# One column block of the mix projection moved ahead of the query, key and value weights in the first half of a prompt: a decoder step on one Trainium2 core

## The chip, the cores and the metric

The program runs on one core of a Trainium2 chip. A core has a TensorE (PE in the profile), a VectorE (DVE), a ScalarE (ACT), a GpSimd (POOL) and a SyncE (SP, which here only issues transfers), each with an instruction stream of its own that it works through in order. The metric is the device time of one execution in microseconds (us); lower is better.

## What is computed

One layer of a hybrid decoder, for a prompt of 1024 tokens and for 8 sequences of 8 new tokens whose attention reads a paged cache of 8192 tokens each. Cut to the parts that matter here:

```
n = rmsnorm(h, g_mix);  u = n @ w_in                       # 1024 -> 1968 columns
gq, gk, gv, gg, ga, mq, mkv, mkr = split(u, [256, 256, 512, 512, 16, 256, 128, 32])
o_gla = gated linear attention of gq, gk, gv, gates from ga; times silu(gg)
qf  = rmsnorm(mq)  @ mla_w_qup     # 256 -> 8 heads x 96, then norms and rope
k,v = rmsnorm(mkv) @ mla_w_kvup    # 128 -> 8 heads x 128
o_mla = attention of the prompt (causal), or of the new tokens over their cached pages
h = h + concat(o_gla, o_mla) @ w_o
h = h + convolutional gated MLP(rmsnorm(h))
h = h + (p @ ple_w_proj) * sigmoid(rmsnorm(h, g_ple) @ ple_w_gate)
```

All of it is float32; matrix products are made of three products of high and low parts (`mm3`, L161), so each weight is cast to a high part (on ACT, L138) and has that subtracted for a low part (L139, on DVE or POOL).

## The kernel before

The program interleaves two streams of work. `cache_stream` (L705) goes over 64 blocks of cached pages. `dense` (L1379) does the prompt: two calls of `prompt_half` (512 tokens each), then the gated linear attention, then the prompt's own attention. The loop at L1636 takes a step from one or from the other: each step of `dense` yields an estimate of its length, and a step of the cache stream is taken whenever its own running sum (4.4 times a factor of `PACE`) is behind. After that a scheduler of the language places the instructions of each engine, so that the two streams are woven together instruction by instruction; a change in the order of the steps therefore moves rows far beyond its own place.

Inside `prompt_half(hf)`, the opening transposes the normed prompt rows into `xTh`, `xTl`, computes the latent columns (`proj_lat`, rows `ps_lt`, kept in `lat`), and, in the first half alone, also the samples' queries: `sample_q` and `q_finish` (L333) turn the product `ps_qs` into normed, rotated queries `qt`; `sample_absorb` transposes those (`pt_q`, L439), multiplies by `WkT` (`ps_qp`, L443) and transposes the rotary part (`pt_qr`, L449). The cache stream can only start when `qp` and `qr` are there.

Then come the parts that the change touches, at L965 to L976:

- `mix(chunks)` (L883): for each column block of 128 columns, `load_mix` reads it in two transfers of 256 KB (`stage<-w_in`), ACT casts both, POOL subtracts both (`lo_eng=pool`). `proj` makes 24 matmuls of 128x512 (`ps_pj`, 8 each of L162, L163 and L164) and ACT copies the sum out (L753). `post` sends it to memory (L850) and, in the first half, makes the samples' columns: 8 matmuls `ps_sm` (L309), an ACT copy (L312), two DVE additions (L313, L315), a transpose (`pt_gvs`, L854) and its copy (L855).
- `rank` transposes the 16 gate columns (`pt_ga`, L869); `norm_latents` norms the latents (L323 on ACT, L131 and L134 on POOL, L326 to L329 and L198 to L201 on DVE).
- `load_q` reads the query weights in four transfers of 192 KB (`stage<-mla_w_qup`), `load_kv` the key and value weights in two of 256 KB (`stage<-mla_w_kvup`); ACT casts them and DVE, not POOL, subtracts (L139, 128x384 and 128x512).
- For each of the four row tiles: `latents_T` (`pt_cq`, L925), then the next column block of `PLAN`, then `heads` (products `ps_q` and `ps_kv`, the norms, and the stores `dq`, `dk`, `dv`).

All weights go through a ring of three buffers named `stage`: a transfer waits until the ACT cast and the subtraction that read the buffer three loads earlier are done. The split weights stand in three buffers `w`; the query weights hold two of them (`wpair`) until the last `heads` of a half.

Of the kernel before, what the change touches and what calls it, by code (L numbers as in the profile page):

```python
# [26 lines left out]
DFF = 2816  # L27
PACE = [1.41, 1.088, 1.601, 1.168, 1.142, 0.708, 1.035, 1.027]
SP = 50
PLAN = ([0], [], [1, 2, 3])  # L30
EARLY = tuple((u // 2, u % 2) for u in range(9))
PASSAGE = (
# [35 lines left out]
def step_kernel(ctx: ExitStack, tc: tile.TileContext, A):  # L68
# [199 lines left out]
    def load_q():  # L268
        return [wload(wp, A["mla_w_qup"][0][:, f * 384:(f + 1) * 384], 2, 384, "w", sbufs=3, out=wpair(2, 384))
                for f in range(2)]  # L270
# [5 lines left out]
    def load_mix(c0, lo_eng=pool):  # L276

        w = wtile().rearrange("p (k s c) -> p k s c", k=8, s=2)
        hl = wload(wp, w_in[:, c0:c0 + P], 8, P, "w", sbufs=3, lo_eng=lo_eng, out=(w[:, :, 0], w[:, :, 1]))
        return hl + (w,)  # L280
# [460 lines left out]
    def prompt_half(hf):  # L741
# [5 lines left out]
        def proj(w, n, st=None):  # L747
            ps = pd([P, 512], "ps_pj")
            for k in range(8):
                mm3(ps[:n], w[0][:, k, :], w[1][:, k, :], xTh[:, k, :], xTl[:, k, :], k == 0, k == 7)  # L750
            if st is None:
                st = wk.tile([P, 512], F32, tag="st", name="st", bufs=3)
            act.copy(st[:n], ps[:n])  # L753
            return st
# [79 lines left out]
        def gates(G, G0):  # L834

            with tc.high_priority():
                for x in [G, ggs] + G0:
                    tc.keep_in_program_order(act.activation(x, x, AF.Silu))
                tc.keep_in_program_order(act.preload_act_table_set("natural_log_exp_and_others"))
            put_gates(G, hs)  # L840
            for x, t in zip(G0, (0, 256)):
                put_gates(x, slice(t, t + 256))
# [4 lines left out]
        def post(c, st, w, G=None):  # L847
            c0 = c * P
            if c < 4:
                sp.dma_start(dgqk[c0:c0 + P, hs], st)  # L850
            if hf == 0:
                t = proj_sample(w, pd)
                pt = pd([P, 512], "pt_gvs")
                pe.transpose(pt[:, :R], t, ident[:R, :R])  # L854
                act.copy(gqT[:, c, :] if c < 4 else ggs[:, c - 8, :], pt[:, :R])  # L855
                if c == 11:
                    put_gates(G, hs)
            elif c == 8:
                for t in (0, 256):
                    x = wk.tile([P, 4, 256], F32, tag="xin", name="G0")  # L860
                    sp.dma_start(x, dgg[:, t:t + 256].rearrange("(c p) t -> p c t", p=P))
                    G0.append(x)
# [3 lines left out]
        def rank():  # L866
            pt = pd([P, 4, P], "pt_ga")
            for i in range(4):
                pe.transpose(pt[:16, i], lat[:, i, 0:16], ident)  # L869
            ga = wk.tile([P, 512], F32, tag="st", name="ga", bufs=3)  # L870
            act.copy(ga[:16], pt[:16].rearrange("p i c -> p (i c)"))
            sp.dma_start(dga[1:17, hs], ga[:16])
            sp.dma_start(dga[0, hs].rearrange("(a b) -> a b", a=4), ones64[0:4])

        def norm_latents(i):
            t = 4 * hf + i
            tt = slice(t * P, (t + 1) * P)
            l = lat[:, i, 16:NL]
            latents(l, P, ropep[:, t, :], l[:, 0:256], l[:, 256:384], l[:, 384:416])
            sp.dma_start(A["ckv_p"][tt, :], l[:, 256:384])  # L880
            sp.dma_start(A["krope_p"][tt, :], l[:, 384:416])

        def mix(chunks, G=None):  # L883
            prev = None
            for c in chunks + [None] * bool(chunks):
                if c is not None:
                    w = load_mix(c * P)
                    st = proj(w, P, G[:, c - 8] if c >= 8 else None)
                    if c == 11 and hf > 0:
                        gates(G, G0)  # L890
                if prev is not None:
                    post(*prev, G)
                prev = (c, st, w)
                yield (5.3 if hf else 7.2) if c is not None else 0.3
# [27 lines left out]
        def latents_T(i):  # L922
            pt = pd([P, 4, P], "pt_cq")
            for c in range(3):
                pe.transpose(pt[:, c, :], lat[:, i, 16 + c * P:16 + (c + 1) * P], ident)  # L925
            cTh = wk.tile([P, 3, P], F32R, tag="u", name="lTh")
            cTl = wk.tile([P, 3, P], F32R, tag="lTl", name="lTl", bufs=1)
            split(cTh, cTl, pt[:, 0:3])
            return cTh, cTl
# [32 lines left out]
            sp.dma_start(dv[tt, :], vt.rearrange("p h c -> p (h c)"))  # L962
            yield 1.3

        yield from mix(PLAN[0])  # L965
        rank()
        for i in range(4):
            norm_latents(i)
        yield from mix(PLAN[1])
        wq = load_q()  # L970
        wkh, wkl = load_kv()
        for i in range(4):
            cT = latents_T(i)
            yield from mix(PLAN[2][i:i + 1])
            yield from heads(i, *cT)
        z["part"] = 2 * hf + 1  # L976
        values(0)
# [401 lines left out]
    def dense():  # L1379
        for hf in range(2):  # L1380
            z["part"] = 2 * hf
            if hf:
                z["gla"] = gla_weights()
            yield from prompt_half(hf)
        den.close()
        wa2 = const.tile([17, 256], F32, tag="gtile", name="wa2")
        sp.dma_start(wa2[0:1], A["gla_b_a"])
        sp.dma_start(wa2[1:17], A["gla_w_a2"][0])
        with ExitStack() as s2:
            g, g2 = (s2.enter_context(tc.tile_pool(name=nm, bufs=2, reuse_waits="tile")) for nm in ("g", "g2"))  # L1390
            z["part"] = 4
            sample = gla_sample(g, wa2, *z["gla"])
            for n, w in enumerate(gla_prompt(g2, wa2, *z["gla"])):
                yield w
                if n > GS0:
                    z["part"] = 5
                    w2 = next(sample, None)
                    if w2 is not None:
                        yield w2
            for w in sample:  # L1400
                yield w
        with ExitStack() as s2:
            ap = s2.enter_context(tc.tile_pool(name="ap", bufs=2, reuse_waits="tile"))
            z["part"] = 6
            yield from prompt_attention(ap)
        z["part"] = 7
        wo_room()
# [1438 lines left out]
```

## Time and profile before

| | us |
|---|---|
| median of 3 runs | 2199.56 (2196.43 to 2205.49) |
| profiled execution, device time | 2198.96 |
| its span in the trace | 2197.3 |
| DVE busy | 1704.0 (78%) |
| ACT busy | 1384.2 (63%) |
| POOL busy | 1229.4 (56%) |

A row of the timeline reads: start, time taken, engine, line, operation, output and input tile with shapes, count; in square brackets the idle time of the engine before it and who ended that. A row of the windows reads: the stretch, its length, busy time of each engine with the number of instructions, then the TensorE clock granted (1.00 is full), the share of the transfer engines and their rate. Transfers in the first 110 us, among them the weights in question, are issued by SP in the order of the program; that order, and the other engines', can be listed from the built program without times.

### The profile page before, as it was taken

The numbers are of one execution on the slowest core, as the hardware profiler recorded it, in microseconds if no ns is written. First come the engines' busy times: TensorE is split into PE (matmuls) and PEld (weight loads), VectorE is DVE, ScalarE is ACT, GpSimd is POOL, SyncE is SP. The second block draws the span as 40 slices with busy tenths as digits, with TensorE's granted clock in tenths as the row PEclk, the third lists the DMA queues.
The fourth block names the chain that finished last, engine by engine and source line by source line (L and its number), as shares of the span: only waits on it lengthen the run. The fifth ranks groups of instructions, "written<-read, shape, count | busy, mean of one in ns | idle before, by whom it ended". The sixth has DMA issues, their size and how long they took to land. (4 is left out here: it accounts for less than half of the span.)

```text
span 2197.3 us, 37407 instructions
## 1 busy us (share of the span) xinstructions
PE 2121.5 (97%) x12928; PEld 1901.9 (87%) x12928; DVE 1704.0 (78%) x2611; ACT 1384.2 (63%) x3735; POOL 1229.4 (56%) x1348
## 2 busy tenths in 40 slices
PE   7999999999999999999999999999999999999998
PEld 6888978878888888887898978999999999888787
DVE  4775667377778888887788888788888886887795
ACT  5676766777778888887777776443333334434761
POOL 6675668576677777767454656556566562011211
PEclk9999999999999999999999999999999999999999
DMA  5343245422342222221431223232322325778642
GB/s 184 109 142 111 72 124 159 131 70 61 104 125 65 61 68 66 62 62 42 164 91 61 68 74 118 90 110 82 98 91 93 100 92 193 221 219 245 195 145 84
DMA packets 203576, 244.55 MB, mean 111 GB/s; under 512 B 42940, under 2 KB 137260, under 8 KB 203388
## 3 DMA queue, kind: packets, MB, share of 16 engines
q1 hardware_dynamic: 184428, 181.39, 26.3%
q0 software_dynamic: 17728, 56.31, 8.7%
q10 hardware_dynamic: 1232, 4.46, 0.6%
q8 instruction: 104, 1.70, 0.3%
q14 instruction: 84, 0.69, 0.1%
HBM read 196.39 MB, written 45.67 MB: 110 GB/s over the span
## 5 line engine op out<-in xcount | busy, mean ns | idle before, releaser
L583 ACT ACTIVATE csq<-ks 128x256 f32<-128x256 f32 x1040 | 392.8, 401 | 93.7 <-PE ks L164 82.0
L588 DVE TENSOR_REDUCE css<-csq 128x16 f32<-128x1024 f32 (+1 forms) x264 | 315.7, 1196 | 60.4 <-ACT csq L583 59.2
L138 ACT CAST wh<-st 128x512 fp32r<-128x512 f32 x164 | 100.9, 619 | 169.9 <-PE ps_gu L163 157.6
L162 PE MATMUL ks<-mv0h,cTh 128*128 128x320 f32 (+1 forms) x520 | 171.5, 332 | 7.4 <-ACT sn L585 3.7
L162 PE MATMUL ks<-mv1h,cTh 128*128 128x320 f32 (+1 forms) x520 | 170.1, 329 | 7.6 <-ACT sn L585 3.6
L628 POOL TENSOR_TENSOR chl<-craw,chl 128x1024 fp32r<-128x1024 f32 x64 | 141.5, 2211 | 55.4 <-ACT chl L626 54.8
L163 PE MATMUL ks<-mv1l,cTh 128*128 128x320 f32 (+1 forms) x520 | 153.8, 298 | 0.0
L163 PE MATMUL ks<-mv0l,cTh 128*128 128x320 f32 (+1 forms) x520 | 152.7, 295 | 0.0
L164 PE MATMUL ks<-mv0h,cTl 128*128 128x320 f32 (+1 forms) x520 | 148.2, 298 | 0.9 <-DVE cTl L139 0.8
L164 PE MATMUL ks<-mv1h,cTl 128*128 128x320 f32 (+1 forms) x520 | 148.4, 299 | 0.1
L656 POOL TENSOR_TENSOR phl<-sn,phl 128x512 fp32r<-128x512 f32 (+1 forms) x63 | 84.0, 1334 | 83.1 <-ACT phl L653 82.6
L139 DVE TENSOR_TENSOR wl<-st,wh 128x512 fp32r<-128x512 f32 x124 | 108.6, 879 | 25.8 <-ACT wh L138 25.7
L139 POOL TENSOR_TENSOR wl<-st,wh 128x512 fp32r<-128x512 f32 x40 | 62.0, 1550 | 104.9 <-ACT wh L138 100.1
L163 PE MATMUL ps_dn<-o 128*128 128x512 f32 x308 | 120.2, 390 | 0.1
L164 PE MATMUL ps_dn<-o 128*128 128x512 f32 x308 | 120.2, 390 | 0.0
L139 DVE TENSOR_TENSOR cTl<-ctp,cTh 128x512 fp32r<-128x512 f32 (+1 forms) x136 | 90.0, 662 | 37.5 <-ACT cTh L138 36.5
L162 PEld LDWEIGHTS ks<-mv0h,cTh 128*128 128x128 f32 x520 | 98.6, 190 | 21.4 <-ACT sn L585 8.1
L585 ACT COPY sn<-ks 128x64 f32<-128x64 f32 x520 | 116.8, 225 | 0.0
L162 PEld LDWEIGHTS ks<-mv1h,cTh 128*128 128x128 f32 x520 | 99.3, 191 | 19.8 <-ACT sn L585 7.4
L1333 POOL TENSOR_TENSOR pl<-p,ph 128x512 fp32r<-128x512 f32 (+1 forms) x96 | 97.5, 1020 | 32.7 <-DVE ph L1332 22.7
L162 PE MATMUL ps_dn<-o 128*128 128x512 f32 x308 | 115.8, 391 | 0.0
L164 PE MATMUL ps_gu<-xrh,wl 128*128 128x320 f32 x352 | 108.8, 309 | 0.0
(744 smaller groups left out, 7760.9 us busy)
## 6 DMA issues: line engine op xcount, KB each, us to landing
raw<-ds SPq DMA_DIRECT2D x77, 256.0 KB
raw<-ffn_w_down SPq DMA_DIRECT2D x66, 256.0 KB
stage<-w_in SPq DMA_DIRECT2D x48, 256.0 KB
wr<-ffn_w_down SPq DMA_DIRECT2D x44, 256.0 KB
st<-ffn_w_gate SPq DMA_DIRECT2D x42, 256.0 KB
st<-ffn_w_up SPq DMA_DIRECT2D x42, 256.0 KB
ds<-cv SPq DMA_DIRECT2D x19, 512.0 KB
oraw<-doT SPq DMA_DIRECT2D x16, 256.0 KB
```

The source lines that it names most:

```text
L138: cast = act.copy(hi, src)
L139: res = (lo_eng or dve).tensor_tensor(lo, src, hi.bitcast(F32), ALU.subtract)
L162: pe.matmul(ps, ah, bh, start=first, stop=False)
L163: pe.matmul(ps, ah, bl, start=False, stop=False)
L164: return pe.matmul(ps, al, bh, start=False, stop=last)
L583: act.activation(sq[:, f * 256:f * 256 + 256], ks[:, 0:256], AF.Square)
L585: act.copy(o.sn[:, g0 + i, :], ks[:, 256:320])
L588: dve.tensor_reduce(o.ss[:, g0 + i + 1 - n:g0 + i + 1, :].rearrange("p i h -> p (i h)"), sq2[:, :n].rearrange("p i (h n) -> p (i h) n", n= ...
L628: pool.tensor_tensor(ch[:, c0:c1, 128:256], src, ch[:, c0:c1, 0:128].bitcast(F32), ALU.subtract)
L656: (dve if drain == 2 else pool).tensor_tensor(phl[:, :nt, 64:128], sb, phl[:, :nt, 0:64].bitcast(F32), ALU.subtract)
L1333: pool.tensor_tensor(pl[:, c0:], p[:, c0:], ph[:, c0:].bitcast(F32), ALU.subtract)
```

## The change

`PLAN` says which column blocks of the mix projection stand at three places of `prompt_half`: ahead of `rank`, between the norms of the latents and `load_q`, and one ahead of each `heads`. It was one table for both halves and is now one for each half. The second half keeps its table. In the first, block 1 moves from the first `heads` to the place ahead of `load_q`, and blocks 2 and 3 move up by one tile.

```
-PLAN = ([0], [], [1, 2, 3])
+PLAN = (([0], [1], [2, 3]), ([0], [], [1, 2, 3]))
...
-        yield from mix(PLAN[0])
+        yield from mix(PLAN[hf][0])
         rank()
         for i in range(4):
             norm_latents(i)
-        yield from mix(PLAN[1])
+        yield from mix(PLAN[hf][1])
         wq = load_q()
         wkh, wkl = load_kv()
         for i in range(4):
             cT = latents_T(i)
-            yield from mix(PLAN[2][i:i + 1])
+            yield from mix(PLAN[hf][2][i:i + 1])
             yield from heads(i, *cT)
```

Every engine has the same instructions before and after; only their order differs. Of the 12,692 matmuls and transposes in PE's order, the 219th is the first that differs and the 6,339th, in the prompt's attention, the last, but for some 20 neighbours that change places much later.

On PE, in the opening, right behind the first column block. The names are: `ps_sm` the samples' columns of block 0, `pt_q` the transposed sample queries, `pt_gvs` the transposed samples' columns, `pt_ga` the gate columns, `ps_pj` a column block's product. Before:

```order
L309 MATMUL ps_sm<-w,xTs 128x256 x4
L439 MATMUL pt_q<-ident,qt 64x64 x8
L854 MATMUL pt_gvs<-ident,gsf 128x64
L869 MATMUL pt_ga<-ident,lat 16x128 x4
L925 MATMUL pt_cq<-ident,lat 128x128 x3
L443 MATMUL ps_qp<-qT_s,WkT 128x64 x8
L162 MATMUL ps_pj<-xTh,w 128x512
L163 MATMUL ps_pj<-xTl,w 128x512
```

and after:

```order
L309 MATMUL ps_sm<-w,xTs 128x256 x4
L439 MATMUL pt_q<-ident,qt 64x64 x8
L854 MATMUL pt_gvs<-ident,gsf 128x64
L869 MATMUL pt_ga<-ident,lat 16x128 x4
L162 MATMUL ps_pj<-xTh,w 128x512
L163 MATMUL ps_pj<-xTl,w 128x512
L164 MATMUL ps_pj<-xTh,w 128x512
L162 MATMUL ps_pj<-xTh,w 128x512
```

Block 1 now begins ahead of `pt_cq` and `ps_qp`: 20 rows of `ps_pj` stand ahead of `ps_qp` where none stood. `pt_q`, `pt_gvs` and `pt_ga` keep their places ahead of block 1.

On DVE, at the same place, the difference in the chain that makes the sample queries `qt` (L123 to L351), with the subtractions of the query weights (`w<-stage`, 128x384) and the samples' columns (`gsf`):

```order
-L139 TENSOR_TENSOR w<-stage,w 128x384 x2
+L139 TENSOR_TENSOR w<-stage,w 128x384
 L123 TENSOR_TENSOR nwt<-qrs 64x16
 L124 SCALAR_TENSOR_TENSOR nwt<-nwt,qss 64x16
 L125 SCALAR_TENSOR_TENSOR qrs<-nwt,qrs 64x16
-L139 TENSOR_TENSOR w<-stage,w 128x384
 L350 TENSOR_TENSOR qt<-qt,qrs 64x8x64
 L353 TENSOR_TENSOR qt<-qt,qrs 64x8x32
+L313 TENSOR_TENSOR gsf<-ps_sm,gsf 64x128
 L351 TENSOR_TENSOR qt<-qt,gqk 64x8x64
```

Of four query-weight subtractions ahead of L351 one is left (the first of the four stood a few rows higher up); one addition of the samples' columns is new there.

On POOL, at the same place, with the cast and subtracted low parts of the column blocks (`w<-stage`), copies for the cache stream (`mv1h`, `mv1l`), and the first cache block's low part (`chl`):

```order
 L496 DMA craw<-cache_ckv,idx 128x1024 x2
+L139 TENSOR_TENSOR w<-stage,w 128x4x128
 L454 CAST mv1h<-mv0h 128x256 x2
-L454 CAST mv1l<-mv0l 128x256 x2
+L454 CAST mv1l<-mv0l 128x256
+L139 TENSOR_TENSOR w<-stage,w 128x4x128
+L454 CAST mv1l<-mv0l 128x256
 L131 TENSOR_SCALAR rs_v<-ss_809 128x3
 L628 TENSOR_TENSOR chl<-craw,chl 128x8x128
```

Both low parts of block 1 now stand ahead of `chl`; before, they stood behind it.

More of the change, by code (lines that the diff above doesn't have):

```diff
@@ L29 @@
 SP = 50
-PLAN = ([0], [], [1, 2, 3])
+PLAN = (([0], [1], [2, 3]), ([0], [], [1, 2, 3]))
 EARLY = tuple((u // 2, u % 2) for u in range(9))
@@ L963, in heads @@
             yield 1.3
-        yield from mix(PLAN[0])
+        yield from mix(PLAN[hf][0])
         rank()
@@ L968, in prompt_half @@
             norm_latents(i)
-        yield from mix(PLAN[1])
+        yield from mix(PLAN[hf][1])
         wq = load_q()
@@ L973, in prompt_half @@
             cT = latents_T(i)
-            yield from mix(PLAN[2][i:i + 1])
+            yield from mix(PLAN[hf][2][i:i + 1])
             yield from heads(i, *cT)
```

## The prediction

> **What bounds the kernel now.** I read the page first, for the engine that sets the pace.
>
> ```profile
> span 2197.3 us, 37407 instructions
> PE 2121.5 (97%) x12928; PEld 1901.9 (87%) x12928; DVE 1704.0 (78%) x2611; ACT 1384.2 (63%) x3735; POOL 1229.4 (56%) x1348
> ```
>
> TensorE is busy for 97% of the span. An edit that removes no TensorE work can gain only from the other 75.8 us (2197.3 − 2121.5) and from time in which the clock is throttled. So the second view is PE's idle time: its waits, longest first (what waited, for whom, total, times, longest).
>
> ```profile
> PE pt L155 <- DVE xin_s L148: 8.6, 1, 8.6
> ...
> PE mt L649 <- DVE mt L646: 5.1, 4, 2.6
> ...
> PE pt_q L439 <- DVE qt L351: 3.6, 1, 3.6
> ...
> PE ps_qp L443 <- ACT qT_s L440: 0.9, 1, 0.9
> ```
>
> The first is the wait for the first input, which nothing here moves. The longest single one after it, `pt_q`, stands exactly where the change cuts in. Third, the windows: one for each 3.4 us around that wait, and four that cut the span at its end, at the end of the slow clock, and where, counted in matmuls, PE's order is about the same again.
>
> ```profile
> 53.93:57.33 3.40, 0.00 (x1) 0.00 (x0) 3.33 (x8) 2.52 (x10) 3.24 (x4) 1.00 0.54 185
> 57.33:60.73 3.40, 2.74 (x16) 1.78 (x16) 3.40 (x12) 1.68 (x8) 1.20 (x2) 0.55 0.51 161
> 60.73:64.13 3.40, 2.91 (x14) 2.92 (x14) 3.31 (x12) 2.42 (x6) 3.06 (x5) 0.50 0.20 42
> 64.13:67.53 3.40, 3.40 (x10) 2.71 (x10) 3.12 (x14) 1.11 (x2) 1.68 (x3) 0.50 0.47 121
> 67.53:70.93 3.40, 3.40 (x22) 2.62 (x21) 1.87 (x6) 0.71 (x2) 2.50 (x11) 0.95 0.32 82
> ...
> 57.55:67.54 9.99, 9.06 (x38) 7.38 (x39) 9.63 (x34) 5.21 (x15) 5.76 (x7) 0.51 0.39 108
> 67.54:1010.00 942.46, 911.83 (x6202) 804.96 (x6201) 699.83 (x1182) 729.40 (x2241) 662.82 (x760) 0.99 0.31 92
> 1010.00:2197.30 1187.30, 1158.40 (x6487) 1052.21 (x6485) 965.60 (x1341) 616.18 (x1394) 525.36 (x524) 0.99 0.39 123
> ```
>
> Two things to see. After the empty stretch the granted clock is 0.51 for 9.99 us, so about 2 × 0.49 × 9.99 = 9.8 us at half speed, worth 4.9 us of work. And two of those three windows are not even full (2.74 and 2.91 of 3.40): what PE runs there is sparse. The place thus costs 3.62 us of waiting, 0.93 at `ps_qp`, and 4.9 of clock: 9.4 us, 0.43% of the span. That is nearly all the change can win where it is made.
>
> **The change, part by part.** It adds and removes nothing: 24 matmuls `ps_pj`, 8 `ps_sm` and their casts only move, so the sum starts at 0 and all terms are waits, clock and order.
>
> *The wait at `pt_q`.* By the order lists `pt_q` stays ahead of block 1 on PE, so the new matmuls can't fill this wait; only the DVE chain behind it can shorten it. That chain before:
>
> ```profile
> 52.36 0.56 DVE L139 TENSOR_TENSOR w<-stage,w 128x384 fp32r<-128x384 f32 x1 [2.55 <-ACT w L138]
> 52.83 2.16 DVE L123 TENSOR_TENSOR nwt<-qrs 64x16 f32<-64x16 f32 x1
> 55.03 0.17 DVE L124 SCALAR_TENSOR_TENSOR nwt<-nwt,qss 64x16 f32<-64x16 f32 x1
> ...
> 55.32 0.55 DVE L139 TENSOR_TENSOR w<-stage,w 128x384 fp32r<-128x384 f32 x1
> 55.79 0.68 DVE L350 TENSOR_TENSOR qt<-qt,qrs 64x512 f32<-64x512 f32 x1
> ...
> 56.73 0.68 DVE L351 TENSOR_TENSOR qt<-qt,gqk 64x512 f32<-64x512 f32 x1
> ```
>
> L123 takes 2.16 us where the like-sized L124 takes 0.17. POOL says why:
>
> ```profile
> 45.97 1.31 POOL L139 TENSOR_TENSOR w<-stage,w 128x512 fp32r<-128x512 f32 x1
> ...
> 48.84 1.79 POOL L496 DMA_INDIRECT craw<-cache_ckv,idx  x1 [0.30 <-issue]
> ...
> 52.48 2.49 POOL L628 TENSOR_TENSOR chl<-craw,chl 128x1024 fp32r<-128x1024 f32 x1
> ```
>
> `chl` runs from 52.48 to 54.97 and L123 ends with it, at 54.99. The two hold each other up. In the new order two subtractions of block 1 (1.31 us each by the row at 45.97) stand ahead of `chl` on POOL, which pushes it to about 52.5 + 2.6 = 55.1, and the subtraction at 55.32 leaves the chain; but L313 enters it, and needs ACT's copy of `ps_sm`. ACT:
>
> ```profile
> 52.23 0.21 ACT L122 ACTIVATE qrs<-qrs 64x16 f32<-64x16 f32 x1
> ...
> 53.79 0.51 ACT L138 CAST w<-stage 128x384 fp32r<-128x384 f32 x1 [0.87 <-DMA stage<-mla_w_qup]
> ...
> 54.68 0.58 ACT L753 COPY st<-ps_pj 128x512 f32<-128x512 f32 x1
> ```
>
> Best case: L122 ends at 52.4 as before; the chain runs free and L313 waits for PE's last `ps_sm` (53.9) and a copy of 0.3, so L351 starts near 54.6 and ends at 55.3, against 57.4 (56.73 + 0.68): 2.1 us won. Worst case: the query weight that ACT still casts ahead of L122 lands later, since block 1's two transfers go ahead of it through the three `stage` buffers (it then comes about as late as the cast at 53.79, 1.4 us behind), and `chl` falls into the chain as it does now: L351 near 58.7, 1.3 us lost. What is late next is `pt_gvs`, right behind `pt_q`: it needs DVE's L315, which now has one more query-weight subtraction (0.55) ahead of it, of a load whose `stage` buffer POOL's first subtraction of block 1 must free; so part of the best case would be waited for there again. I take **0.5 won**, the middle, because both ends rest on which of two engines is a few tenths earlier.
>
> [...]
>
> *The wait at `ps_qp`.* It waits 0.93 us for ACT's copy of `pt_q`. Now 20 matmuls of `ps_pj` stand between.
>
> ```profile
> 61.22 3.67 PE L443 MATMUL ps_qp<-qT_s,WkT 64*128 64x64 f32 x16 [0.93 <-ACT qT_s L440]
> ...
> 65.41 0.63 PE L163 MATMUL ps_pj<-xTl,w 128*128 128x512 f32 x1
> 65.83 0.63 PE L164 MATMUL ps_pj<-xTh,w 128*128 128x512 f32 x1
> ...
> 71.07 0.40 PE L162 MATMUL ps_pj<-xTh,w 128*128 128x512 f32 x1
> 71.31 0.40 PE L163 MATMUL ps_pj<-xTl,w 128*128 128x512 f32 x1
> ```
>
> Start to start they take 0.42 us in the slow clock and 0.24 in the full one, so 20 cover 5 to 8 us. ACT's copy now stands behind two casts of query weights, which come two loads later than before; even 4 us more fit under the cover. **0.9 won**; if the cover is gone, 0.
>
> *The clock.* Dense 512-wide matmuls now follow where sparse small ones stood. Other stalls show what a stall costs when dense work follows:
>
> ```profile
> 351.66 0.69 PE L649 MATMUL mt<-ident,bm 64*128 64x64 f32 x2 [2.64 <-DVE mt L646]
> 437.30 0.66 PE L1022 MATMUL ps_z<-wa,gaT 17*128 17x256 f32 x2 [2.42 <-DMA Ss<-state_gla]
> 654.50 0.42 PE L162 MATMUL ks<-mv1h,cTh 128*128 128x320 f32 x1 [1.26 <-ACT cTh L138]
> 350.00:359.00 9.00, 7.34 (x33) 6.93 (x34) 5.64 (x15) 4.61 (x13) 5.53 (x8) 0.62 0.98 286
> 436.00:444.00 8.00, 6.70 (x44) 5.67 (x44) 4.85 (x7) 5.95 (x20) 5.09 (x6) 1.00 0.86 239
> 654.00:660.00 6.00, 5.50 (x30) 4.99 (x31) 4.01 (x8) 3.19 (x11) 5.68 (x7) 0.72 0.76 232
> ```
>
> After the stall at 351.66 the mean of 0.62 over 9 us is 2 × 0.38 × 9 = 6.8 us at half speed. The one of 1.26 us at 654.50 also led to a slow stretch (0.72 in the row from 654 on), while the one of 2.42 at 437.30 did not (1.00). So a stall of about 2.6 us may or may not throttle. I take 6.8 us in place of 9.8, **1.5 won** (half of the 3.0), with 0 and 4.9 as the ends.
>
> *The other queues.* On SP block 1's two transfers pass four of query weights and two of key and value weights, 1.25 MB; those come later by two loads. The last of them and their first use were
>
> ```profile
> 62.02 1.13 ACT L138 CAST wkv<-stage 128x512 fp32r<-128x512 f32 x2
> 76.99 0.45 PE L162 MATMUL ps_q<-w,lTh 128*128 128x384 f32 x1
> ```
>
> so some 14 us lie between, and the first `heads` now stands behind block 2 and more cache work, which covers the two loads; without that cover two late loads would cost PE about 2 us, at the 0.87 that one load costs ACT in the row at 53.79. The rest of ACT's and DVE's opening (L198 to L446, `pt_qr`) is due at block 1's end, 5 to 8 us on.
>
> *The reshuffle.* The order differs on every engine up to about 1010 us. Between 67.54 and there PE idles 942.46 − 911.83 = 30.6 us and loses about 9 to the clock (0.99, rounded): some 40 us in about 20 stalls of 0.5 to 2.6 us, drawn anew. I cost it at **0**, since neither sign follows from any row, and by the spread of 20 such stalls give it 8 us either way.
>
> **Sum.** 0.5 + 0.9 + 1.5 = 2.9 won (ends: 7.9 won, 1.3 lost). The profiled execution took 2199.0 (span 2197.3 and 1.7 around it), 0.6 below the median of 2199.56. 2199.0 − 2.9 = 2196.1; I predict **2196**.
>
> **Rivals.**
> - *The clock stays up.* The stall falls to 1.5 us and PE isn't throttled: all 7.9 won, **2191**. For it: the 2.42 us stall without a slow stretch. Against: the 1.26 us one with it. [...] Chance 0.2.
> - *Nothing won here.* `chl` blocks the chain again, the same wait, the same clock: **2199 to 2200**. For it: the wait stands ahead of the moved block. Chance 0.25.
> - *The reshuffle takes stalls away.* Two of the kind at 351.66 (2.64 plus 3.4 of clock, 6.0) vanish besides the 2.9: **2184**. Chance 0.12.
> - *Slower: the cache stream's maximum comes late.* `mt` (L649) must wait for DVE's L646 in each block. If DVE's woven order puts dense work ahead of L646 in some blocks, each costs those 6.0 us; only 4 waits of this kind exist now. Three more give 2199 − 2.9 + 18 = **2214**; with two it is 2208, still within; the third decides. For it: DVE is 78% busy and its order is drawn anew. Against: there are 4 such waits now, 5.1 us in all. Chance 0.08.
> - The forecast keeps 0.35.
>
> **How the numbers follow.** The local ends (2191 and 2200) with half of the reshuffle's 8 us added give 2187 to 2204; to take in half of what lies between there and the two outer rivals I widen it to **2185 to 2206**. Faster by over 0.5% (about what a measurement of this kernel can tell from no change) means below 2188.6: the reshuffle rival, and a quarter of the first, **0.17**. Slower means above 2210.6: **0.08**. Within: **0.75**.
>
> **What would show it.** In the new profile: the wait `pt_q` between 1.5 and 3.6 us, with L123 short and `chl` behind L351; no wait at `ps_qp`; one slow stretch of about 7 us, with `ps_pj` in it; the stretch from there to about 1010 with idle time of 31 ± 8 us. I am wrong if `pt_q` waits longer than 4 us, if PE waits for `w<-stage` of query weights, or if the gain or loss beyond 8 us lies in the woven part.

## The result, and the profile after

The changed kernel takes 2214.11 us (median of 7 runs, 2210.62 to 2222.16); the one before, run beside it, 2196.97 (7 runs, 2195.19 to 2205.49; the three of the table above are among them). The ratio is 1.0072, 95% interval 1.0051 to 1.0092: slower by some 16 us, where 2196 was forecast and 2206 was the upper end. The profiled execution took 2210.98 us, 12.0 more than that of before. Its page:

```profile
span 2209.0 us, 37427 instructions
PE 2123.2 (96%) x12928; PEld 1902.4 (86%) x12928; DVE 1705.6 (77%) x2611; ACT 1381.1 (63%) x3735; POOL 1228.8 (56%) x1348
```

TensorE is busy for 1.7 us more, and idle for 85.8 us (2209.0 − 2123.2) where it was 75.8. Over the whole span nearly all of the difference is waiting. PE's waits by line, longest first:

```profile
PE ks L162 <- ACT sn L585: 8.7, 14, 1.9
PE pt L155 <- DVE xin_s L148: 8.1, 1, 8.1
PE pt_q L439 <- DVE qt L351: 5.0, 1, 5.0
PE ps_z L1022 <- DMA gaT<-dga: 4.3, 1, 4.3
...
PE mt L649 <- DVE mt L646: 3.9, 3, 2.2
PE o L1341 <- POOL pl L1333: 3.6, 3, 1.6
PE pt_cq L925 <- ACT qt L343: 3.2, 1, 3.2
```

`pt_q` has grown from 3.6 to 5.0, and `ps_qp` is gone from the list. `mt`, the slower rival of the forecast, waits less than before (3.9 against 5.1). `ps_z` waits 4.3 us, for the load of `gaT`, where it waited 2.42 for another load. `o` and `pt_cq` are new in the list. All three stand far behind the place of the change: `pt_cq` at 348 us, `ps_z` at 447, the two longest waits of `o` at 754 and 895.

The opening, on PE, DVE and POOL:

```profile
58.63 1.03 PE L439 MATMUL pt_q<-ident,qt 64*64 64x64 f32 x8 [4.96 <-DVE qt L351]
...
66.35 2.00 PE L443 MATMUL ps_qp<-qT_s,WkT 64*128 64x64 f32 x16
```

```profile
52.49 1.48 DVE L139 TENSOR_TENSOR w<-stage,w 128x384 fp32r<-128x384 f32 x1 [3.29 <-ACT w L138]
53.89 0.36 DVE L123 TENSOR_TENSOR nwt<-qrs 64x16 f32<-64x16 f32 x1
...
54.69 2.67 DVE L350 TENSOR_TENSOR qt<-qt,qrs 64x512 f32<-64x512 f32 x1
...
57.82 0.67 DVE L351 TENSOR_TENSOR qt<-qt,gqk 64x512 f32<-64x512 f32 x1
```

```profile
52.26 1.29 POOL L139 TENSOR_TENSOR w<-stage,w 128x512 fp32r<-128x512 f32 x1
...
54.65 2.17 POOL L628 TENSOR_TENSOR chl<-craw,chl 128x1024 fp32r<-128x1024 f32 x1
```

`chl` did move back on POOL by 2.2 us, as the forecast said, but DVE's chain did not get past ahead of it: DVE's L139, with a subtraction of block 1 beside it on POOL from 52.26 to 53.55, took 1.48 us where the same row took 0.56, and `chl` then falls on L350 (2.67 in place of 0.68), not on L123. The query weight was not late: ACT's L122, behind its cast, stands at 52.37 where it stood at 52.23. The clock, in windows:

```profile
57.07:60.47 3.40, 1.83 (x13) 1.38 (x14) 3.40 (x11) 1.58 (x8) 3.18 (x4) 0.50 0.26 70
60.47:63.87 3.40, 3.40 (x12) 2.77 (x11) 3.34 (x12) 2.41 (x11) 1.10 (x2) 0.67 0.61 169
63.87:67.27 3.40, 3.40 (x19) 2.62 (x19) 2.91 (x18) 0.54 (x1) 1.38 (x2) 1.00 0.45 125
...
58.63:67.00 8.37, 8.37 (x39) 6.47 (x39) 7.85 (x31) 3.72 (x12) 4.18 (x6) 0.76 0.48 128
```

The slow stretch, at the 0.50 that the first of these windows shows, is 2 × 0.24 × 8.37 = 4.0 us, where it was 9.8. At the place of the change itself the sum is thus: `pt_q` 1.3 lost (4.96 − 3.62), `ps_qp` 0.9 won, clock (9.8 − 4.0) / 2 = 2.9 won, together 2.5 won. So the 12 us come from elsewhere. One more landmark: the first `ks` that waits for ACT's `csq` in the prompt's attention, in before and after:

```profile
1061.98 0.41 PE L162 MATMUL ks<-mv0h,cTh 128*128 128x320 f32 x1 [1.37 <-ACT csq L583]
```

```profile
1075.36 0.41 PE L162 MATMUL ks<-mv0h,cTh 128*128 128x320 f32 x1 [1.36 <-ACT csq L583]
```

There the new kernel is 13.4 us late, more than the whole difference of the spans (11.7; the stretch behind this row took 1131 to 1136 us in 19 of the 20 traces, so a difference of 2 us there says nothing). All of the loss is made ahead of about 1060 us, which is the stretch whose order the scheduler has drawn anew; behind it the orders are all but the same. The windows from the end of the slow clock to this row, in before and after:

```profile
67.54:1061.98 994.44, 957.98 (x6478) 843.55 (x6476) 735.03 (x1235) 766.15 (x2340) 699.23 (x803) 0.99 0.30 90
```

```profile
67.00:1075.36 1008.36, 964.31 (x6479) 848.94 (x6477) 736.60 (x1241) 764.60 (x2342) 698.70 (x802) 0.98 0.30 88
```

For the same number of matmuls this stretch takes 13.9 us longer: PE is idle for 7.6 us more (44.1 against 36.5) and busy for 6.3 us more, at a granted clock of 0.98 in place of 0.99, both rounded. So here the loss is waiting in about half, and the rest is the same work taking longer.

### The profile page after: what moved, and what is told of

Same layout as the page of the kernel before. It is cut to its first block, busy times and chain, and to the rows that moved or that the text cites. A ratio compares the mean times of both kernels' runs of the same rounds, so it can differ in the third digit from the quotient of the medians.

```text
span 2209.0 us, 37427 instructions
## 1 busy us (share of the span) xinstructions
PE 2123.2 (96%) x12928; PEld 1902.4 (86%) x12928; DVE 1705.6 (77%) x2611; ACT 1381.1 (63%) x3735; POOL 1228.8 (56%) x1348
## 5 line engine op out<-in xcount | busy, mean ns | idle before, releaser
L628 POOL TENSOR_TENSOR chl<-craw,chl 128x1024 fp32r<-128x1024 f32 x64 | 140.7, 2198 | 50.8 <-ACT chl L626 50.2
L139 DVE TENSOR_TENSOR wl<-st,wh 128x512 fp32r<-128x512 f32 x124 | 108.7, 879 | 26.3 <-ACT wh L138 26.1
L139 POOL TENSOR_TENSOR wl<-st,wh 128x512 fp32r<-128x512 f32 x40 | 62.6, 1564 | 103.0 <-ACT wh L138 103.0
L139 DVE TENSOR_TENSOR cTl<-ctp,cTh 128x512 fp32r<-128x512 f32 (+1 forms) x136 | 90.0, 662 | 31.8 <-ACT cTh L138 31.4
L615 POOL TENSOR_TENSOR sn<-sn,cy 128x512 f32<-128x512 f32 (+1 forms) x64 | 71.2, 1112 | 70.6 <-DVE cy L613 58.9
```

The costliest lines, as they stand in the source:

```text
L139: res = (lo_eng or dve).tensor_tensor(lo, src, hi.bitcast(F32), ALU.subtract)
L615: pool.tensor_tensor(snv, snv, y[:, :nt].rearrange("p i h -> p (i h)").unsqueeze(2).broadcast_to([P, nt * 8, 8]), ALU.mult)
L628: pool.tensor_tensor(ch[:, c0:c1, 128:256], src, ch[:, c0:c1, 0:128].bitcast(F32), ALU.subtract)
```

## The experiments

Two theories stood at the start. W: the later weave, drawn anew, makes the loss. O: the opening makes it. To part them the order of issue was pinned: a kernel is built twice, once with each `PLAN`, the scheduled order of each is read, and a third build, a graft, gets the first CUT instructions in one order and the rest in the other, by a dependency that orders each instruction behind the one before it on its engine and waits for no data. 1000 instructions reach to about 110 us, 4500 to about 446, 6500 to about 583. The edit, on top of the changed kernel, for the first graft (the functions `traced` and `ordered`, which pin and read an order, are left out here):

```
+def build(arrays):
+    head, tail = ordered(arrays, HEAD), ordered(arrays, TAIL)
+    first = set(head[:CUT])
+    return traced(arrays, TRACED, head[:CUT] + [k for k in tail if k not in first])[0]
+TRACED, HEAD, TAIL, CUT = AFTER, AFTER, BEFORE, 1000
```

All times are medians. Each ratio is to the kernel before, run beside it (medians of 2196 to 2200 us), with its 95% interval; it is not the quotient of the two medians, and can differ from that by 0.1%. Pinning by itself costs nothing that these runs can tell: c_chl_last, below, is pinned all through in the order of before, but for one POOL instruction, and takes 0.9996 of its time.

**g_open_after**: the changed opening, before's order behind it.

> A graft. Every engine runs the first 1000 scheduled instructions (about 110 us) in the order of the changed kernel, with block 1 ahead of the loads and blocks 2 and 3 one tile earlier, and all others in the order that they have in the kernel before. Theory W (the loss lies in the later weave, which the scheduler drew anew): as the kernel before, 2194 to 2200 us, although the wait at pt_q is near 5 us as in the changed kernel. Theory O (the loss is made by the opening: block 1 ahead delays query, key and value weights and the dense work falls behind): as the changed kernel, 2209 to 2216.

Measured: 2204.82 us, 1.0029 (1.0016 to 1.0041): between the ranges of W and O, nearer to W's.

**g_open_before**: the reverse (`BEFORE, BEFORE, AFTER, 1000`).

> The reverse graft: the first 1000 scheduled instructions in the order of the kernel before (block 1 behind the loads), all others in the order that they have in the changed kernel. Theory W: slow like the changed kernel, 2209 to 2216. Theory O: like the kernel before, 2194 to 2200.

Measured: 2217.12 us, 1.0072 (1.0057 to 1.0087): the whole loss without the changed opening. W carries; the opening has a few us at most.

**g_block_ahead**: block 1 ahead of the loads, blocks 2 and 3 where they were, the opening alone (`MOVED, MOVED, BEFORE, 605`).

> Block 1 alone is ahead of the loads: the first 605 scheduled instructions (to the end of block 1) come from a program with block 1 ahead and blocks 2 and 3 at their old tiles, all later ones stand in the order of the kernel before. Theory W: 2194 to 2200, the wait at pt_q 4 to 5 us, the slow clock after it near 7 us. Theory O: slower than before by 8 us or more.

Measured: 2203.7 us, 1.0015 (1.0006 to 1.0025), `pt_q` 4.94. That is above W's range and below O's. So with the changed opening in front of before's order 0.1 to 0.3% are lost, although the terms at the place itself came to a gain; whether by the opening or by the joint between two orders, these runs do not tell. By a row that before has at 654.50 us (it stands in the prediction) this kernel is 6.3 us late, and a wait for POOL that before does not have stands soon behind the opening, as the timeline of PE shows:

```profile
79.76 0.58 PE L163 MATMUL csr<-qbd0l,kTh 128*128 128x256 f32 x1 [2.81 <-POOL qbd0l L514]
...
660.79 0.42 PE L162 MATMUL ks<-mv1h,cTh 128*128 128x320 f32 x1 [1.26 <-ACT cTh L138]
```

**n_kvfirst**: before, with two loads swapped and no block moved.

```
-        wq = load_q()
         wkh, wkl = load_kv()
+        wq = load_q()
```

> The kernel before with load_kv called ahead of load_q: no column block moves, two loads swap, and the scheduler weaves all that follows anew. Theory W: anywhere from 2190 to 2215, with a change of some us against the kernel before although nothing of the mix projection moved. Theory O: within 3 us of the kernel before.

Measured: 2215.48 us, 1.0064 (1.0048 to 1.0079). The wait at `pt_q` vanishes (2.78 us of it come back at the next transpose, `pt_gvs`), and the kernel is as slow as the changed one. An edit that has nothing to do with the blocks brings a loss of the same size.

**Where in the weave?** W1: ahead of 446 us, where the changed kernel waits 4.3 us for `ps_z`. W2: behind.

**w_after_4500** (`AFTER, AFTER, BEFORE, 4500`) and **w_before_4500** (`BEFORE, BEFORE, AFTER, 4500`).

> The changed kernel's own order for the first 4500 scheduled instructions (to about 446 us, past the start of the linear attention), the order of before for the rest. Theory W1 (the weave's loss is made ahead of 446 us, by stalls like ks behind cTl at 142 us and ps_z behind the load of gaT): as slow as the changed kernel, 2211 to 2217 us, with ps_z waiting about 4 us for gaT. Theory W2 (the loss is made behind 446 us, by o waiting for POOL's pl at 754 to 895 us): only the opening's 3 to 6 us and the few of 120 to 200 us remain, 2202 to 2207 us, and the waits o behind pl are gone. Rival O is out by the earlier runs.

> The reverse: before's order for the first 4500 scheduled instructions, the changed kernel's for the rest. W1: near before, 2198 to 2203 us. W2: 2206 to 2212 us, with the waits o behind POOL's pl (1.6 us each) seen again. If both this one and its mirror lie between, the loss is spread over the whole weave and neither stretch holds it alone.

Measured: 2201.7 us, 1.0017 (1.0006 to 1.0027), and 2213.34 us, 1.0071 (1.0056 to 1.0086). W2, more clearly than expected: the changed order behind 446 us makes about the whole loss by itself, 16.4 us. (With the 4.8 us of the other graft that is more than the whole; the shares of two grafts do not add up exactly.) The timeline of w_after_4500 shows why the eye was misled by `ps_z`:

```profile
445.05 1.22 PE L1022 MATMUL ps_z<-wa,gaT 17*128 17x256 f32 x2 [2.91 <-DMA gaT<-dga]
...
1064.64 0.41 PE L162 MATMUL ks<-mv0h,cTh 128*128 128x320 f32 x1 [1.36 <-ACT csq L583]
```

It reaches `ps_z` 7.75 us later than before (445.05 against 437.30) and with a longer wait, and stands only 2.7 us behind at the landmark. By the start of `ps_z` PE had made 2562 matmuls in this kernel and 2510 in before, with 410.2 and 403.9 us of busy time. So about 6 of the 7.75 us are work taken earlier, not time lost. PE's timeline in w_before_4500:

```profile
439.53 0.67 PE L1022 MATMUL ps_z<-wa,gaT 17*128 17x256 f32 x2 [2.32 <-DMA Ss<-state_gla]
...
458.69 0.44 PE L523 MATMUL crp<-ident,krraw 128*128 128x128 f32 x2 [1.28 <-DVE pvs L679]
...
480.46 0.42 PE L164 MATMUL csr<-qbd0h,kTl 128*128 128x64 f32 x1 [1.08 <-DVE kTl L139]
...
757.74 0.50 PE L1341 MATMUL o<-pl,vo 128*128 128x512 f32 x1 [1.55 <-POOL pl L1333]
...
898.45 0.39 PE L1341 MATMUL o<-pl,vo 128*128 128x256 f32 x1 [1.62 <-POOL pl L1333]
...
1079.54 0.42 PE L162 MATMUL ks<-mv0h,cTh 128*128 128x320 f32 x1 [1.37 <-ACT csq L583]
```

Windows of before, and then of w_before_4500:

```profile
437.00:583.00 146.00, 141.55 (x1019) 118.40 (x1020) 106.40 (x189) 108.22 (x353) 100.74 (x145) 1.00 0.29 82
583.00:760.00 177.00, 171.70 (x1215) 149.70 (x1213) 143.85 (x236) 145.55 (x447) 135.61 (x158) 0.99 0.31 87
760.00:1060.00 300.00, 291.46 (x1977) 254.54 (x1977) 243.34 (x396) 255.09 (x753) 219.64 (x220) 0.99 0.21 58
```

```profile
437.00:583.00 146.00, 135.98 (x939) 111.86 (x937) 102.06 (x174) 101.58 (x336) 98.18 (x142) 0.98 0.27 77
583.00:760.00 177.00, 169.97 (x1200) 147.65 (x1200) 138.89 (x235) 139.78 (x439) 128.99 (x153) 0.99 0.31 89
760.00:1060.00 300.00, 288.29 (x1957) 252.06 (x1956) 239.69 (x400) 251.61 (x746) 219.50 (x219) 0.98 0.21 59
```

PE is busy for 5.6, 1.7 and 3.2 us less, 10.5 in all, and by the granted clock (1.00 to 0.98, and 0.99 to 0.98, both rounded) loses about 3 us more in the first and 3 in the last, an estimate (146 × 0.02 and 300 × 0.01): some 16 us, in many waits of up to 1.6 us. The landmark says about the same: this kernel is 2.2 us late at `ps_z` and 17.6 at the landmark.

**One stretch or both?** V1: the linear attention from 446 to 583 us. V2: `o` behind POOL's `pl`, later. **v_before_6500** (`BEFORE, BEFORE, AFTER, 6500`) and **v_mid**, which has before's order but for the instructions 4500 to 6500:

```
+    pin = head[:CUT] + [k for k in tail if k not in first]
+    first = set(pin[:6500])
+    return traced(arrays, TRACED, pin[:6500] + [k for k in head if k not in first])[0]
+TRACED, HEAD, TAIL, CUT = BEFORE, BEFORE, AFTER, 4500
```

> Before's order for the first 6500 scheduled instructions (to about 583 us), the changed kernel's behind. The loss of the weave lies behind 446 us by the runs before. Theory V1 (the linear attention from 446 to 500 us makes it: PE waits there for pvs, csr and ps_z's followers, and the clock falls): back to 2198 to 2204 us, although o still waits for POOL's pl twice by 1.6 us. Theory V2 (o behind pl, at 754 and 895 us, makes it): 2206 to 2212 us. If it lies between, both have a share.

> Before's order all through, but for the instructions 4500 to 6500 (446 to 583 us), which stand in the changed kernel's order. V1: 2206 to 2213 us, with waits of 1 us and more at crp (for pvs) and csr (for kTl) and a clock of about 0.94 from 440 to 500 us. V2: 2197 to 2202 us. The two runs should add up to about 13 to 16 us above before between them.

Measured: 2207.71 us, 1.0059 (1.0044 to 1.0073), and 2205.77 us, 1.0045 (1.0032 to 1.0058). Each stretch has a share, and neither theory stands alone. In v_mid the two waits of the first stretch are there and those of `o` are not:

```profile
455.96 0.44 PE L523 MATMUL crp<-ident,krraw 128*128 128x128 f32 x2 [1.29 <-DVE pvs L679]
...
477.74 0.42 PE L164 MATMUL csr<-qbd0h,kTl 128*128 128x64 f32 x1 [1.07 <-DVE kTl L139]
```

In v_before_6500 it is the other way round:

```profile
751.17 0.50 PE L1341 MATMUL o<-pl,vo 128*128 128x512 f32 x1 [1.55 <-POOL pl L1333]
...
892.03 0.39 PE L1341 MATMUL o<-pl,vo 128*128 128x256 f32 x1 [1.75 <-POOL pl L1333]
```

The two come to 9.3 + 11.3 = 20.6 us above before, where 13 to 16 were expected and the whole is 16.4; a joint between two orders may have a price of its own, which these runs do not part from the rest.

**The collision at `pt_q`.** **c_chl_behind** is g_block_ahead with POOL's first `chl` moved behind two pairs of the norm; **c_chl_before** does the same to before, **c_chl_last** moves it in before still further back, behind the third mix subtraction. The edit (`pin` is the whole order, `pool` POOL's part of it, `chl` the first L628 there; in c_chl_last, `late` is the third L139 of `load_mix`):

```
+    late = [k for k in pool if k[-2:] == (("rstd", "134"), 2) and ("latents", "325") in k and ("prompt_half", "968") in k]
+    pin.remove(chl)
+    pin.insert(pin.index(late[0]) + 1, chl)
```

> Block 1 ahead of the loads in the opening, all else in before's order, as in g_block_ahead, and in addition POOL's first chl subtraction (L628) moved behind two L131/L134 pairs, so that it no longer stands beside DVE's chain to pt_q. If the collision of chl with L350 (2.67 us where the other kernel has 0.68) makes the longer wait: L350 about 0.7 us, pt_q waits about 2.9 us instead of 4.94, and the time falls by 2 to 4 us against g_block_ahead, to 2200 to 2202 us. If the late query weights make it, L350 is short but pt_q still waits over 4 us and the time stays at 2203 to 2205 us. If chl was due where it stood, a new wait appears in the cache stream behind it.

> The kernel of before in its own order, with that one chl subtraction moved behind the two L131/L134 pairs. If L123 (2.16 us) was long because of chl: L123 about 0.2 to 0.4 us, pt_q waits about 1.6 us instead of 3.6, and the time is 2 to 4 us below before (ratio 0.998 to 0.999). If the wait is only handed on (pt_gvs or ps_qp behind it are late too): the same time as before within 1 us.

> The kernel of before in its own order, with POOL's first chl subtraction moved behind the third subtraction of a mix weight (it then runs at about 61 us, behind DVE's L351). If the collision with chl is what makes this wait: L123 0.2 us, L350 0.7 us, pt_q waits about 1.6 us instead of 3.6, 2194 to 2196 us, ratio 0.998 to 0.999. If nothing is won though pt_q is short, the wait was handed on, to pt_cq or ks (the norm's rs_r and the cache stream stand behind chl on POOL).

Measured: c_chl_behind 2201.23 us, 1.0015 (1.0005 to 1.0024). DVE and PE:

```profile
54.95 0.68 DVE L350 TENSOR_TENSOR qt<-qt,qrs 64x512 f32<-64x512 f32 x1
...
58.17 2.40 DVE L198 TENSOR_TENSOR rqa<-qt,ropes 64x256 f32<-64x256 f32 x1
```

```profile
56.92 1.03 PE L439 MATMUL pt_q<-ident,qt 64*64 64x64 f32 x8 [2.96 <-DVE qt L351]
```

c_chl_before 2198.95 us, 1.0008 (0.9999 to 1.0018):

```profile
53.60 0.16 DVE L123 TENSOR_TENSOR nwt<-qrs 64x16 f32<-64x16 f32 x1
...
55.86 2.65 DVE L350 TENSOR_TENSOR qt<-qt,qrs 64x512 f32<-64x512 f32 x1
```

```profile
59.59 1.03 PE L439 MATMUL pt_q<-ident,qt 64*64 64x64 f32 x8 [4.98 <-DVE qt L351]
```

c_chl_last 2196.04 us, 0.9996 (0.9984 to 1.0008). L351 runs free. It ends at 55.78 and is what `pt_q` waits for (the releaser that PE's row names was done by about 55.0):

```profile
55.10 0.68 DVE L351 TENSOR_TENSOR qt<-qt,gqk 64x512 f32<-64x512 f32 x1
```

```profile
55.93 0.60 PE L439 MATMUL pt_q<-ident,qt 64*64 64x64 f32 x8 [2.38 <-ACT junk L323]
...
60.24 3.67 PE L443 MATMUL ps_qp<-qT_s,WkT 64*128 64x64 f32 x16 [1.57 <-ACT qT_s L440]
```

What makes the wait long is shown: wherever `chl` stands beside the chain, the DVE instruction that it meets takes 2.2 to 2.7 us, and `pt_q` waits 2.4 to 3.0 us where `chl` meets none ahead of it, 3.6 with L123 held and 5.0 with L350. (In c_chl_before not all of the 5.0 is `chl`: a wait of DVE of 1.22 us for ACT's cast of a query weight stands in the chain too.) The price for the kernel is not what was expected: with `chl` out of the chain the time did not fall in either kernel (1.0015 as in g_block_ahead, 0.9996). In c_chl_last, of 1.24 us won at `pt_q`, 0.64 went on to `ps_qp` (1.57 in place of 0.93), and the slow clock stayed: 0.63 over the 4.31 us from `pt_q` on, then 7.03 us at 0.50 behind the wait at `ps_qp`, as the windows show. What is left is less than the interval can tell.

```profile
60.24:67.27 7.03, 7.03 (x24) 6.24 (x25) 6.25 (x15) 3.04 (x7) 6.79 (x10) 0.50 0.25 65
```

**Is it the draw, or the blocks?** A draw is an order that the scheduler makes anew after an edit. **e_move_only** moves block 1 alone and leaves all else to the scheduler (one list for each of the first three tiles; the line that reads the lists is changed to fit):

```
+PLAN = (([0], [1], [[], [2], [3]]), ([0], [], [[1], [2], [3]]))
```

> A second natural redraw: only block 1 goes ahead of the loads in the first half, blocks 2 and 3 keep their places at the second and third tile, and the scheduler orders all else by itself. If every redraw is a draw of its own around some mean that lies above before (before is a lucky draw): anywhere from 2197 to 2217 us, in no relation to the opening, which is that of the changed kernel (pt_q 4.9 us). If instead the changed kernel's loss comes from blocks 2 and 3 standing a tile earlier: back to 2201 to 2205 us, the opening's price alone.

Measured: 2196.23 us, 0.9998 (0.9986 to 1.0011), below both ranges, with the changed kernel's wait in the opening:

```profile
58.10 1.03 PE L439 MATMUL pt_q<-ident,qt 64*64 64x64 f32 x8 [4.94 <-DVE qt L351]
...
1063.65 0.42 PE L162 MATMUL ks<-mv0h,cTh 128*128 128x320 f32 x1 [1.33 <-ACT csq L583]
```

So the opening with block 1 ahead need not cost anything in the end. But it could still have been that blocks 2 and 3, a tile earlier, cost the 16 us (B), and not the draw (D). Three redraws: the changed kernel and e_move_only with the loads swapped as in n_kvfirst (**r_after_kv**, **r_move_kv**), and the changed kernel with the loads called ahead of block 1 (**e_loadsfirst**):

```
-        yield from mix(PLAN[hf][1])
         wq = load_q()
         wkh, wkl = load_kv()
+        yield from mix(PLAN[hf][1])
```

> The changed kernel with the key and value loads called ahead of the query loads: all three mix blocks stand as in the changed kernel, and the scheduler draws everything else anew. Theory D (the loss is the draw): the time may land anywhere from 2196 to 2218 us; under 2206 us speaks for D. Theory B (blocks 2 and 3 standing a tile earlier make the loss): 2210 to 2217 us, as the changed kernel.

> The kernel with block 1 alone moved ahead (e_move_only, 2196 us), with the key and value loads called ahead of the query loads. D: anywhere from 2196 to 2218 us; over 2204 us speaks for D, since no block stands otherwise than there. B: 2194 to 2200 us, as e_move_only, because blocks 2 and 3 are in their old places.

> Blocks 1, 2 and 3 in the changed kernel's stages, but all three loads ahead of block 1's, so that the opening's queues (the query weights first) are as in before. D: anywhere from 2196 to 2218 us, pt_q waiting 1.5 to 4 us. B: 2207 to 2215 us, since blocks 2 and 3 stand a tile earlier.

Measured: 2212.13 us, 1.0068 (1.0054 to 1.0082); 2212.4 us, 1.0071 (1.0057 to 1.0085); 2215.2 us, 1.0082 (1.0068 to 1.0096). The first and the third fit both theories. r_move_kv decides: it is 16 us above e_move_only with all blocks where they are there, and B falls. But every slow kernel so far had the loads swapped, or blocks 2 and 3 early (P). The last three add neither edit; they call the norms of the four row tiles in another order, in before (**r_before_norm**), in e_move_only (**r_move_norm**) and in the changed kernel (**r_after_norm**):

```
-        for i in range(4):
+        for i in (1, 0, 2, 3):
             norm_latents(i)
```

> The kernel of before with nothing but the calls of norm_latents in the order 1, 0, 2, 3: no block moves, no load is swapped. Theory D (each redraw is a draw, and before's is a good one): slower than before by up to 16 us, 2205 to 2217 us, as five of the six other redraws were. Theory P (what costs is the loads swapped, or blocks 2 and 3 a tile early, either one bringing the same slow weave): 2194 to 2200 us, as before, since neither is done.

> e_move_only (2196 us) with the same reordered norm_latents calls. D: anywhere from 2196 to 2217 us; over 2204 us speaks for D. P: 2193 to 2200 us, as e_move_only.

> The changed kernel with the same reordered norm_latents calls. D: anywhere from 2196 to 2217 us; under 2206 us speaks for D. P: 2209 to 2217 us, as the changed kernel, since blocks 2 and 3 stand a tile early.

Measured: 2213.81 us, 1.0075 (1.0058 to 1.0093); 2203.12 us, 1.0023 (1.0013 to 1.0033); 2206.47 us, 1.0038 (1.0025 to 1.0052). D holds, by the first of them: before loses 16.6 us by an edit that changes nothing but the order of two calls, where P allowed 2200 at most. The edit's own effect in the opening is small (`ps_qp` waits 1.77 us in place of 0.93, `pt_q` as before). The other two lie outside P's ranges but just short of the marks set for D (2204 and 2206). The changed kernel wins about 7.5 us by the same edit (2214.1 against 2206.5). PE's timeline of r_before_norm at the landmark:

```profile
1076.35 0.42 PE L162 MATMUL ks<-mv0h,cTh 128*128 128x320 f32 x1 [1.36 <-ACT csq L583]
```

The ten orders that the scheduler made, by time: 2196.2 (e_move_only), 2197 (before), 2203.1, 2206.5, 2212.1, 2212.4, 2213.8, 2214.1 (the change), 2215.2, 2215.5. The six with block 1 ahead of the loads run from 2196.2 to 2214.1, the four without from 2197 to 2215.5: by these ten, the place of block 1 says nothing about the time.

No version beat the kernel before: c_chl_last and e_move_only are the same as it within their intervals.

## Why the prediction was wrong

- *The frame held.* The edit adds no work (PE's busy time moved by 0.1%), and the place itself had little to give.
- *`pt_q`, 0.5 won with ends 2.1 won and 1.3 lost:* it landed on the losing end, 1.34 lost, by half of the mechanism named for it: not the late query weight (ACT's L122 stood 0.14 us later), but `chl` in the chain. Beside it L350 took 2.67 us; without it, in before and in c_chl_behind, 0.68. What made L139 ahead of it take 1.48 us in place of 0.56 was not tested apart. The rows of L123 (2.16 us) and `chl` showed such a collision already, and the forecast should have gone by the 1.3 lost of its worst case, in which `chl` falls into the chain. But the chl runs show that these us, once removed, do not come back in the total.
- *`ps_qp`, 0.9 won:* right; no wait is left.
- *The clock, 1.5 won:* right in sign, too small; 2.9 won, since the slow stretch fell to 4.0 us and not 6.8. That the 512-wide `ps_pj` shorten it, which now start 1.9 us behind the stall and not 7.3 (60.52 behind 58.63, 64.81 behind 57.55), was the author's estimate; it fits these two traces, and no run tests it apart.
- *The local sum* of 2.9 won was 2.5 in the trace. That it came so near is luck: 1.8 too much at `pt_q` and 1.4 too little at the clock nearly cancel. The grafts with this opening lose 0.1 to 0.3% all the same; one wait seen there (in g_block_ahead `csr` behind POOL's `qbd0l`, 2.8 us) had no term, since the forecast's "other queues" counts the weights and the rest of the opening, and not the cache stream behind it.
- *The step that failed* is the reshuffle: "I cost it at **0**, since neither sign follows from any row, and by the spread of 20 such stalls give it 8 us either way." The order behind 446 us, drawn anew, costs 16.4 us by itself (w_before_4500). Both the centre and the size were off. The size was set at 8 of some 40 us of idle time and slow clock; in the changed kernel that stretch came out 13.9 us longer, 7.6 of them idle and 6.3 busy with the same work. Of nine other orders eight are slower than before, by 6 to 17 us, and one is equal: before is a favourable order, and an edit that redraws it was more likely to lose than to win. That could not be read from before's rows; a redraw by an edit with hardly any effect of its own shows it. Two of the forecast's own signs of being wrong came up: `pt_q` over 4 us, and a loss beyond 8 us in the woven part.
- *The slower rival* had the size (2214) by luck, with the wrong place: `mt` behind L646 did not lengthen. Its chance of 0.08 was that of one mechanism, where the loss came from many small waits at once.

Which property makes an order good or bad stays open. For the changed kernel the runs name waits behind 446 us (`crp`, `csr`, `o`) and the clock, and show that two stretches share the loss; they do not show why the scheduler finds the better order only sometimes. These waits are no mark of a slow order: e_move_only has them too (`csr` 1.00 us at 462, `crp` 1.17 at 473, `o` 1.74 at 1036) and loses nothing, while r_before_norm, 16.6 us slower than before, has no wait at `crp`, `csr` or `o` of 1 us or more between 446 us and the landmark. Where the other slow orders lose their time was not tested by grafts. Nor is it shown why before's order is among the best; the factors of `PACE`, with three decimals each, may have been fitted to it, and no run tests that.

## What to carry to other kernels

Where a scheduler weaves two streams, an edit is two things: its own effect, and a new draw of everything behind it. Before a small gain is credited to the one or a loss to the other, redraw both kernels by an edit with next to no effect of its own (two calls swapped) and see how far the times scatter; here that scatter was 19 us, and what the edit itself could give was 3. Pinning the order of one part tells where a loss lies, and a landmark that both kernels pass at the same amount of work tells more than the longest wait on the list.

## What the runs showed of the hardware that had not been expected

- How long the clock stayed slow did not go by the length of the stall: behind 4.96 us of waiting at `pt_q` in the changed kernel 4.0 us at the clock of 0.50, behind 3.62 in before 9.8, and in c_chl_last, behind 2.38 and then 1.57 at `ps_qp`, 10.2 (2 × 0.37 × 4.31 = 3.2, and 7.03). In c_chl_last PE was busy for all of the 3.60 us of `ps_qp`, whose matmuls are 64 wide, and the clock stayed at 0.50; by the windows it rose only about 3.5 us after the first 512-wide `ps_pj` (at 63.84). In before it rose about 3.1 us after that matmul (at 64.81), in the changed kernel about 2.2 us after it (at 60.52), which there starts 1.9 us behind the stall. These are three traces and no rule. Nor did the slow stretch at 655 us follow one stall of 1.26 us alone, as the prediction has it: from 650.80 to 655.00 us PE in before was busy for 2.66 of 4.20 us, at a clock of 1.00, and from 655 to 660 the clock was 0.66. The window of `ps_qp` in c_chl_last, then that of the first `ps_pj` in the changed kernel:

```profile
60.24:63.84 3.60, 3.60 (x17) 3.48 (x17) 3.58 (x6) 1.93 (x5) 3.36 (x5) 0.50 0.37 96
```

```profile
60.52:62.60 2.08, 2.08 (x7) 1.69 (x6) 2.02 (x5) 1.98 (x10) 0.05 (x1) 0.50 0.75 223
```

- The DVE instructions that `chl` met were held by about the same time, whatever their own length: 0.16 became 2.16 (L123), 0.68 became 2.67 (L350), and 0.41 became 2.40 (L198), about 2.0 us more each time; `chl` itself takes 2.2 us in the mean (64 of them in before), and took 2.49 beside L123 and 2.17 beside L350, so that the prediction's "hold each other up" is shown for DVE's side alone. Moving `chl` moved the collision to another DVE instruction in each of the three orders tried (in c_chl_last to L199, 0.16 to 2.20).
